# Sixteen more gate halves between the stick-breaking turns, two casts on another engine, four gate halves at a stage switch

## The chip, the cores and the metric

The kernel runs as one program on one core of a Trainium2 chip. The number that counts is the device time of one execution in microseconds. Three runs of the kernel before took 2511.12, 2511.8 and 2515.66 us, so the median is 2511.8 us. Everything is fp32, but each large product is computed from three fp32r products of a high and a low half (below), so one logical matmul is three instructions on TensorE.

## The reference, cut to what matters

The model is two blocks one after the other. The first (windowed attention, a gated delta rule, an FFN) is not touched. The second, `hybrid_layer`, normalizes, projects `h` to eleven pieces, runs three mixers, and merges them with three sigmoid gates:

```
h = rms_norm(x, g_pre);  u = h @ w_in            # 1024 tokens, 1024 -> 5120 + 3 * 1024 columns
y_pool = pool_mixer(pool_v) * silu(pool_g)       # branch one,   1024 x 512
y_conv = conv_mixer(conv_x, ...) * silu(conv_g)  # branch two,   1024 x 512
y_sb   = stick_breaking(q, k, v) * silu(sb_g)    # branch three, 1024 x 512
proj   = branches[n] @ w_branch[n]               # 512 -> 1024, for n = 0, 1, 2
merged = sum over n of sigmoid(merge[n]) * proj[n]
out    = x + rms_norm(merged @ w_out, g_post)
```

`merge` is the last 3 * 1024 columns of `u`: one gate of 1024 x 1024 for each branch. A gate depends on `h` alone, not on its branch, so it can be computed at any time after `h`. Stick-breaking attention walks for each of 8 heads over blocks of 128 keys from the last to the first and needs at each block the sum of the blocks after it, so it is a chain:

```
logits = q @ k * scale;  log_keep = where(mask, log_sigmoid(-logits), 0)
later  = reversed cumsum of log_keep, less log_keep
weights = where(mask, exp(log_sigmoid(logits) + later), 0);  out = weights @ v
```

## The kernel before, in words

Matrices stand transposed: a tile has 128 rows of features and 512 tokens, and a "half" is one of the two runs of 512 tokens. A weight tile of 128 x 512 is loaded by `weight` (line 103: the DMA on SyncE's queue, line 106), split into a high part `wh` (a cast) and a low part `wl` (a subtraction on GpSimd), and used by `mm3` (lines 147 to 149), three matmuls of 128 x 128 by 128 x 512. A flag, `busy[0]`, says which engine casts: ScalarE outside the stick-breaking stage (line 98), VectorE inside it (line 109).

Two stages matter here.

**The stick-breaking stage.** Sixteen streams (`stream`: 8 heads, each for two halves of the queries) run two at a time in turns. A stream has 4 or 8 key blocks, together 96, and a block passes `logits` (two matmuls into `l`, then copy, Abs, Exp and Ln on ScalarE, line 990 on VectorE), `closing` (lines 998, 1000 and 1001 on VectorE), `sums` (two matmuls into `S`), `weights` (VectorE adds at line 1011, ScalarE takes Exp at line 1012, VectorE casts to `uh` at line 1014, GpSimd subtracts to `ul` at line 1015) and `values` (two matmuls into `O`). A block is 128, 256, 384 or 512 queries wide; 48 of the 96 have all 512. Between turns the generator `others` gives TensorE other work in steps of three matmuls of 512 columns: the projections and activations of branches one and two, the gate of stick-breaking and, for `AHEAD` = 8 tiles of 128 gate rows (two halves each), the whole gate of branch one, which goes to DRAM (`ga_d`). That makes 576 steps, and 8 more sets of three in the pooling epilogue. There are 272 turns; the first 24 steps and the last 24 stand apart, and the others are spread evenly over the turns:

```
while turn[1] and done < LEAD + (t + 1) / len(turns) * (total - LEAD - SPARE):
    next(fill, None)
```

TensorE's order in this stage is as written. The order of all other engines, and TensorE's elsewhere, comes from the framework's scheduler.

**The merge stage.** For each branch `n`, eight tiles `Y[k, h]` (4 blocks of 128 features, two halves) are loaded through two `yr` buffers, for `n` = 2 multiplied by the gate `sg_d` on GpSimd (line 1188, with both buffers in use), and split into high and low (ScalarE line 98, VectorE line 99). Their pool holds ten pairs: eight in use and two ahead. Then for each of 8 row tiles `m` and two halves: a gate half (24 matmuls, and a sigmoid: ScalarE lines 156, 158, 159, VectorE line 157) or, for branch one, a load of it from `ga_d` into `s` (line 1198); then 12 matmuls of `Y`; then VectorE multiplies by the gate, and for `n` > 0 GpSimd adds to the sum (line 1212). In all, 16 x 12, 16 x 36 and 16 x 36 matmuls for the three branches. SyncE issues all loads in one queue, in order.

Of the kernel before, what the change touches and what calls it, by code (L numbers as in the profile page):

```python
# [9 lines left out]
F32 = mybir.dt.float32  # L10
# [7 lines left out]
P = 128  # L18
# [38 lines left out]
def tile_hybrid_layers(ctx, tc, a, out):  # L57
    nc = tc.nc
    act, dve, gp, pe, sp = nc.scalar, nc.vector, nc.gpsimd, nc.tensor, nc.sync
    dma = sp.dma_start  # L60
# [36 lines left out]
    def split(H, L, src, eng=None):  # L97
        act.copy(H, src)  # L98
        (eng or dve).tensor_sub(L, src, f32(H))  # L99

    busy = [False]

    def weight(src, n=1):

        raw = wp.tile([P, 512], F32, name="raw", tag="raw", bufs=3)
        dma(raw.rearrange("p (k m) -> p k m", k=n), src.rearrange("(k p) m -> p k m", p=P))
        H, L = (wp.tile([P, 512], F32R, name=f"w{q}", tag=f"w{q}", bufs=8) for q in "hl")
        if busy[0]:
            dve.tensor_copy(H, raw)  # L109
            gp.tensor_sub(L, raw, f32(H))  # L110
        else:
            split(H, L, raw, gp)
        return H, L
# [4 lines left out]
    def cols(W, c0, n, K=8):  # L118

        g = [weight(W[k * P : (k + n) * P, c0 : c0 + 512 // n], n) for k in range(0, K, n)]  # L120

        def tile_of(k, m):
            c = (k % n) * (512 // n) + m * P
            return tuple(x[:, c : c + P] for x in g[k // n])

        return tile_of
# [18 lines left out]
    def mm3(ps, A, B, first, last, asl=slice(None), bsl=slice(None)):  # L145

        pe.matmul(ps, A[0][:, asl], B[0][:, bsl], start=first, stop=False)  # L147
        pe.matmul(ps, A[0][:, asl], B[1][:, bsl], start=False, stop=False)  # L148
        pe.matmul(ps, A[1][:, asl], B[0][:, bsl], start=False, stop=last)  # L149

    def acc512():
        return pm[0].tile([P, 512], F32, name="mm", tag="mm")

    def sigmoid(s, x):

        act.activation(s, x, AF.Exp, scale=-1.0)
        dve.tensor_scalar(s, s, 1e18, 1.0, op0=ALU.min, op1=ALU.add)
        act.activation(s, s, AF.Ln)
        act.activation(s, s, AF.Exp, scale=-1.0)
# [176 lines left out]
    raw = wp.tile([P, 512], F32, name="raw", tag="raw", bufs=3)  # L336
# [6 lines left out]
    ps = bank()  # L343
# [7 lines left out]
    for h in range(2):  # L351
        ps = acc512()
# [28 lines left out]
    ps = bank()  # L381
# [10 lines left out]
    ps = bank()  # L392
# [38 lines left out]
    for c in range(8):  # L431
        kT = chunk_of(gk_d, c, "kT")
        ps = bank()
# [17 lines left out]
        b = up_tile("b", 2)  # L451
# [7 lines left out]
    for d in range(2):  # L459
# [3 lines left out]
        for b in range(4):  # L463
            r = slice(32 * b, 32 * b + 32)
# [4 lines left out]
        for s in range(1, 32):  # L469
            i = 31 - s if d == 0 else s  # L470
            r = slice(i + 1, 32) if d == 0 else slice(0, i)
            m = M.rearrange("p a b -> p (a b)")[:, : s * s].rearrange("p (a b) -> p a b", a=s)
# [3 lines left out]
        for b in range(4):  # L476
            r = slice(32 * b, 32 * b + 32)
# [9 lines left out]
    ps = bank()  # L487
# [15 lines left out]
    for c in (0, 7, 1, 6, 2, 5, 3, 4):  # L503
        vT = chunk_of(gv_d, c, "kT")
        ps = bank3()
# [7 lines left out]
    for c in (0, 7, 1, 6, 2, 5, 3, 4):  # L513
        kT, qT = chunk_of(gk_d, c, "kT"), chunk_of(gq_d, c, "qT")
        ps = bank2()
# [161 lines left out]
    for kv in range(2):  # L677
# [8 lines left out]
        for n in range(8):  # L686
# [12 lines left out]
            for h in range(4):  # L699
                ps = acc512()  # L700
# [21 lines left out]
            for b in range(nb):  # L722
                ps = bank()
                for h in range(4):
                    pe.transpose(ps[:, hs(h)], S[:, h, hs(b)], ident)
                H, L = (ap_.tile([P, 512], F32R, name="PT", tag="PT", bufs=4) for _ in range(2))
# [21 lines left out]
    for n in range(2):  # L748
        g = [rows(WO, k, 512 * n) for k in range(4)]
        for i in range(8):  # L750
# [4 lines left out]
            ps = acc512()  # L755
# [96 lines left out]
    HH = kts(HU)  # L852
# [111 lines left out]
    def stream(hd, half):  # L964

        r = slice(64 * hd, 64 * hd + 64)
        qc = slice(512 * half, 512 * half + 512)
        (K, V), Q = heads[hd], queries[hd, half]
        kbs = list(range(4 * half + 3, -1, -1))
        N = len(kbs)  # L970
        cut = [slice(max(0, P * kb - 512 * half), 512) for kb in kbs]
        st = {}

        def logits(j):

            kb, cs = kbs[j], cut[j]
            l = pl.tile([P, 512], F32, name="l", tag="l")
            for n in range(2):
                pe.matmul(l[:, cs], K[:, P * kb : P * kb + P], Q[n][:, cs], start=n == 0, stop=n == 1)
            u, e = ct("u", bufs=5), ct("e", bufs=3)  # L980
            c = cs.start
            if kb >= 4 * half:
                dve.tensor_add(u[:, c : c + P], l[:, c : c + P], neg2)
                c += P
            if c < 512:
                act.copy(u[:, c:], l[:, c:])
            act.activation(e[:, cs], u[:, cs], AF.Abs)
            act.activation(e[:, cs], e[:, cs], AF.Exp, scale=-1.0)
            act.activation(e[:, cs], e[:, cs], AF.Ln, bias=one)
            dve.scalar_tensor_tensor(e[:, cs], u[:, cs], 0.0, e[:, cs], op0=ALU.max, op1=ALU.add)  # L990
            st[j] = u, e

        def closing(j):

            (u, e), cs = st[j], cut[j]
            if j:
                cp = cut[j - 1]
                dve.tensor_sub(e[96:97, cp], e[96:97, cp], Sb[0][0:1, cp])
            eH, eL = ct("eh", F32R, EB), ct("el", F32R, EB)
            dve.tensor_copy(eH[:, cs], e[:, cs])  # L1000
            dve.tensor_sub(eL[:, cs], e[:, cs], f32(eH[:, cs]))
            st[j] = u, (eH, eL)

        def sums(j):
            Sb[0] = pS.tile([P, 512], F32, name="S", tag="S")
            for n, x in enumerate(st[j][1]):
                pe.matmul(Sb[0][:, cut[j]], upto, x[:, cut[j]], start=n == 0, stop=n == 1)

        def weights(j):
            u, cs = st[j][0], cut[j]  # L1010
            dve.tensor_add(u[:, cs], u[:, cs], Sb[0][:, cs])
            act.activation(u[:, cs], u[:, cs], AF.Exp)
            uH, uL = ct("uh", F32R), ct("ul", F32R)
            dve.tensor_copy(uH[:, cs], u[:, cs])  # L1014
            gp.tensor_sub(uL[:, cs], u[:, cs], f32(uH[:, cs]))  # L1015
            st[j] = st[j] + ((uH, uL),)

        def values(j):
            for x in st.pop(j)[2]:
                pe.matmul(Ob[:, cut[j]], V[:, kbs[j]].rearrange("p s d -> p (s d)"), x[:, cut[j]], start=False, stop=True,  # L1020
                          skip_group_check=True)

        Sb = [None]
        logits(0)
        yield
        yield
        for j in range(1, N + 1):
            closing(j - 1)
            if j < N:
                logits(j)  # L1030
            yield
            if j == 2:
                Ob = pO.tile([P, 512], F32, name="O", tag="O")
                dve.memset(Ob, 0.0)
            if j >= 2:
                values(j - 2)
            sums(j - 1)
            weights(j - 1)
            yield
        values(N - 1)  # L1040
        t = tmp()
        act.copy(t[0:64], Ob[64:128])
        dve.tensor_add(t[0:64], t[0:64], Ob[0:64])
        put(ys_d[r, qc], t[0:64])
# [25 lines left out]
            gp.tensor_mul(x, x, y)  # L1070
        put(dst, x)

    AHEAD, LEAD, SPARE = 8, 24, 24
    ga_d = scratch("ga_d", [AHEAD * P, T])

    def others():
# [98 lines left out]
    yp = pool(s7, "y")  # L1175
    gt = pool(s7, "gt")
    ac = pool(s7, "acc", 16)
    A = {}
    for n in range(3):
        Y = {}  # L1180
        for h in range(2):
            for k in range(4):
                raw = gt.tile([P, 512], F32, name="yr", tag="yr", bufs=2)
                dma(raw, y_d[n][k * P : (k + 1) * P, 512 * h : 512 * h + 512])
                if n == 2:
                    raw2 = gt.tile([P, 512], F32, name="yr", tag="yr", bufs=2)
                    dma(raw2, sg_d[k * P : (k + 1) * P, 512 * h : 512 * h + 512])
                    gp.tensor_mul(raw, raw, raw2)  # L1188
                Y[k, h] = tuple(yp.tile([P, 512], F32R, name="y", tag="y", bufs=20) for _ in range(2))
                split(*Y[k, h], raw)  # L1190
        for m in range(8):
            ahead = n == 0 and m < AHEAD
            gw = None if ahead else cols(W2, 5120 + 1024 * n + P * m, 4)
            bw = cols(a["w_branch_2"][0][n], P * m, 4, K=4)
            for h in range(2):
                s = gt.tile([P, 512], F32, name="s", tag="s", bufs=4)
                if ahead:
                    dma(s, ga_d[m * P : (m + 1) * P, 512 * h : 512 * h + 512])
                else:
                    ps = acc512()  # L1200
                    for k in range(8):
                        mm3(ps, gw(k, 0), HH[k][h], k == 0, k == 7)
                    sigmoid(s, ps)
                ps = acc512()
                for k in range(4):
                    mm3(ps, bw(k, 0), Y[k, h], k == 0, k == 3)
                if n == 0:
                    A[m, h] = ac.tile([P, 512], F32, name="a", tag="a")
                    dve.tensor_mul(A[m, h], ps, s)
                else:  # L1210
                    dve.tensor_mul(s, ps, s)  # L1211
                    gp.tensor_add(A[m, h], A[m, h], s)  # L1212
# [60 lines left out]
```

## Time and profile before

| | |
|---|---|
| median of three runs | 2511.8 us |
| the profiled execution | 2522.66 us, span 2520.9 us, mean granted clock 0.983 |
| TensorE busy | 2384.3 us (95%), 11098 matmuls |
| VectorE, ScalarE, GpSimd busy | 1285.9, 1074.3, 928.8 us |
| stick-breaking stage | from about 1542 to 2119 us |
| merge stage | 2119 to about 2425 us |
| output projection and final norm | to the end |

Times in rows are microseconds from the span's start. PE is TensorE, PEld its weight loads, DVE VectorE, ACT ScalarE, POOL GpSimd, SP SyncE; a `q` behind an engine's name is its instruction queue. A matmul row's duration is from its start to the end of its last result, so rows of consecutive matmuls overlap.

### The profile page before, as it was taken

What the parts mean: (1) busy time and instruction counts of PE and PEld (TensorE: products, weight loads), DVE (VectorE), ACT (ScalarE), POOL (GpSimd) and SP (SyncE); (2) the same over time, 40 slices, a digit from 0 to 9 for tenths busy, and PEclk for the clock granted to TensorE, in tenths of its full rate; (3) what the DMA queues carried; (4) which work ended last, traced back from release to release, by engine and by line L of the source; (5) the groups of instructions that cost most, each with busy time, mean ns of one, the idle gap of its engine ahead of it and who ended that gap; (6) DMA issues with size and microseconds to landing.
All of it is one profiled execution on the core that took longest, in us unless ns stands there. A gap on an engine that the chain in (4) does not pass through costs nothing. (4 is left out here: it accounts for less than half of the span.)

```text
span 2520.9 us, 31629 instructions
## 1 busy us (share of the span) xinstructions
PE 2384.3 (95%) x11098; PEld 1954.2 (78%) x11098; DVE 1285.9 (51%) x2481; ACT 1074.3 (43%) x2185; POOL 928.8 (37%) x799
## 2 busy tenths in 40 slices
PE   7899888899999999999999999998999999999998
PEld 5677677887788888888888788777777787888887
DVE  5579936885632211221123504999888885312113
ACT  5554215664542233223224423666555575333331
POOL 3344224434332222222223214455444442345354
PEclk9999988999999999999999999999999999999999
DMA  5895795656221111111112324122222225312123
GB/s 164 226 286 170 214 289 159 195 150 203 73 69 57 42 43 51 50 50 51 50 51 92 103 89 121 57 76 66 66 67 64 71 80 171 113 51 84 51 72 121
DMA packets 307282, 268.47 MB, mean 106 GB/s; under 512 B 44871, under 2 KB 240387, under 8 KB 307123
## 3 DMA queue, kind: packets, MB, share of 16 engines
q1 hardware_dynamic: 264403, 213.41, 29.6%
q10 hardware_dynamic: 42720, 53.05, 6.1%
q8 instruction: 87, 1.43, 0.2%
q14 instruction: 72, 0.59, 0.1%
HBM read 203.92 MB, written 64.57 MB: 107 GB/s over the span
## 5 line engine op out<-in xcount | busy, mean ns | idle before, releaser
L99 POOL TENSOR_TENSOR wl<-raw,wh 128x512 fp32r<-128x512 f32 x276 | 370.8, 1355 | 834.8 <-ACT wh L98 808.9
L147 PE MATMUL mm<-uh,wh 128*128 128x512 f32 x1472 | 578.3, 393 | 0.2 <-DVE mx L1066 0.2
L149 PE MATMUL mm<-uh,wl 128*128 128x512 f32 x1472 | 576.9, 392 | 0.0
L148 PE MATMUL mm<-ul,wh 128*128 128x512 f32 x1472 | 576.4, 392 | 0.0
L98 ACT CAST wh<-raw 128x512 fp32r<-128x512 f32 (+1 forms) x277 | 169.9, 618 | 460.9 <-PE mm L149 239.3
L149 PEld LDWEIGHTS mm<-uh,wl 128*128 128x128 f32 x1472 | 277.7, 189 | 59.5
L147 PEld LDWEIGHTS mm<-uh,wh 128*128 128x128 f32 x1472 | 278.1, 189 | 55.0 <-DVE mx L1066 0.6
L148 PEld LDWEIGHTS mm<-ul,wh 128*128 128x128 f32 x1472 | 277.8, 189 | 55.4
L99 DVE TENSOR_TENSOR hid<-t,hid 128x512 fp32r<-128x512 f32 x64 | 55.4, 866 | 310.1 <-ACT hid L98 310.1
L149 PE MATMUL mm<-wh,hid 128*128 128x512 f32 x512 | 199.0, 389 | 0.0
L148 PE MATMUL mm<-wl,hid 128*128 128x512 f32 x512 | 198.8, 389 | 0.0
L147 PE MATMUL mm<-wh,hid 128*128 128x512 f32 x512 | 198.7, 389 | 0.0
L845 DVE TENSOR_TENSOR h<-h,mm 128x512 f32<-128x512 f32 x128 | 87.9, 687 | 212.3 <-PE mm L149 212.2
L1015 POOL TENSOR_TENSOR ul<-u,uh 128x512 fp32r<-128x512 f32 (+3 forms) x96 | 106.1, 1106 | 134.5 <-DVE uh L1014 108.5
L147 PE MATMUL mm<-xnh,wh 128*128 128x512 f32 x352 | 142.6, 405 | 11.1 <-ACT cv L280 5.8
L110 POOL TENSOR_TENSOR wl<-raw,wh 128x512 fp32r<-128x512 f32 x72 | 101.6, 1411 | 120.7 <-DVE wh L109 45.2
L148 PE MATMUL mm<-xnl,wh 128*128 128x512 f32 x352 | 141.8, 403 | 0.0
L149 PE MATMUL mm<-xnh,wl 128*128 128x512 f32 x352 | 141.4, 402 | 0.0
L148 PEld LDWEIGHTS mm<-wl,hid 128*128 128x128 f32 x512 | 96.1, 188 | 20.0
L147 PEld LDWEIGHTS mm<-wh,hid 128*128 128x128 f32 x512 | 96.1, 188 | 20.0
L149 PEld LDWEIGHTS mm<-wh,hid 128*128 128x128 f32 x512 | 96.1, 188 | 19.9
L830 ACT ACTIVATE t<-mm 128x512 f32<-128x512 f32 x64 | 38.2, 597 | 149.8 <-PE mm L149 149.8
(331 smaller groups left out, 4616.3 us busy)
## 6 DMA issues: line engine op xcount, KB each, us to landing
raw<-in_w_in SPq DMA_DIRECT2D x172, 256.0 KB
raw<-in_w_ffn_in SPq DMA_DIRECT2D x64, 256.0 KB
raw<-in_w_ffn_out SPq DMA_DIRECT2D x64, 256.0 KB
e<-e_d SPq DMA_DIRECT2D x16, 512.0 KB
raw<-in_w_out SPq DMA_DIRECT2D x32, 256.0 KB
kv<-kv_d SPq DMA_DIRECT2D x16, 512.0 KB
kT<-gk_d SPq DMA_DIRECT2D x30, 256.0 KB
raw<-in_w_branch SPq DMA_DIRECT2D x24, 256.0 KB
```

Source lines behind the costliest of these rows:

```text
L98: act.copy(H, src)
L99: (eng or dve).tensor_sub(L, src, f32(H))
L110: gp.tensor_sub(L, raw, f32(H))
L147: pe.matmul(ps, A[0][:, asl], B[0][:, bsl], start=first, stop=False)
L148: pe.matmul(ps, A[0][:, asl], B[1][:, bsl], start=False, stop=False)
L149: pe.matmul(ps, A[1][:, asl], B[0][:, bsl], start=False, stop=last)
L830: act.activation(t, ps, AF.Relu)
L845: dve.tensor_add(Hs[order[p], n], Hs[order[p], n], ps)
L1015: gp.tensor_sub(uL[:, cs], u[:, cs], f32(uH[:, cs]))
```

## The change

`AHEAD` goes from 8 to 16: the stick-breaking stage also computes the whole gate of branch two and stores it in `ga_d`, and the merge stage loads it. In that stage the cast of `weight` alternates between VectorE and ScalarE, and the cast to `uh` moves to ScalarE. At the start of the merge stage, behind the splits of branch one's `Y`, four gate halves of branch three (row tiles 0 and 1) are computed and kept in four `se` buffers until branch three uses them.

```diff
-    busy = [False]
+    busy = [False, False]
...
         if busy[0]:
-            dve.tensor_copy(H, raw)
+            busy[1] = not busy[1]
+            dve.tensor_copy(H, raw) if busy[1] else act.copy(H, raw)
             gp.tensor_sub(L, raw, f32(H))
...
             uH, uL = ct("uh", F32R), ct("ul", F32R)
-            dve.tensor_copy(uH[:, cs], u[:, cs])
+            act.copy(uH[:, cs], u[:, cs])
...
-    AHEAD, LEAD, SPARE = 8, 24, 24
+    AHEAD, LEAD, SPARE = 16, 24, 24
...
+    def gate(gw, h, tag, bufs):
+        s = gt.tile([P, 512], F32, name="s", tag=tag, bufs=bufs)
+        ps = acc512()
+        for k in range(8):
+            mm3(ps, gw(k, 0), HH[k][h], k == 0, k == 7)
+        sigmoid(s, ps)
+        return s
+
+    EARLY = (2, 0), (2, 1)
...
+        if n == 0:
+            for b, m in EARLY:
+                gw = cols(W2, 5120 + 1024 * b + P * m, 4)
+                for h in range(2):
+                    E[b, m, h] = gate(gw, h, "se", 4)
         for m in range(8):
-            ahead = n == 0 and m < AHEAD
-            gw = None if ahead else cols(W2, 5120 + 1024 * n + P * m, 4)
+            ahead = 8 * n + m < AHEAD
+            gw = None if ahead or (n, m) in EARLY else cols(W2, 5120 + 1024 * n + P * m, 4)
...
                 if ahead:
-                    dma(s, ga_d[m * P : (m + 1) * P, 512 * h : 512 * h + 512])
+                    s = gt.tile([P, 512], F32, name="s", tag="s", bufs=4)
+                    r = (8 * n + m) * P
+                    dma(s, ga_d[r : r + P, 512 * h : 512 * h + 512])
                 else:
-                    ps = acc512()
-                    for k in range(8):
-                        mm3(ps, gw(k, 0), HH[k][h], k == 0, k == 7)
-                    sigmoid(s, ps)
+                    s = E[n, m, h] if gw is None else gate(gw, h, "s", 4)
```

The first place is ScalarE's queue in the stick-breaking stage. Before, it holds the Exp of `weights` (L1012) among the passes for the next logits (`e`) and the fill's sigmoid (`mx`):

```order
L988 ACTIVATE e_14988<-e_14988 128x512
L1012 ACTIVATE u_14896<-u_14896 128x384
L989 ACTIVATE e_14988<-e_14988,cc_75 128x512
L158 ACTIVATE mx_15001<-mx_15001 128x512
L986 COPY u_15035<-l_15032 128x256
```

Now the cast to `uh` (L1015) and a weight cast (L110) stand in the same queue:

```order
L1013 ACTIVATE u_13029<-u_13029 128x384
L990 ACTIVATE e_13145<-e_13145,cc_75 128x512
L1015 CAST uh_13165<-u_13029 128x384
L110 CAST wh_13655<-raw_13653 128x512
L157 ACTIVATE mx_13207<-mm_13132 128x512
```

The Exp and the cast of one block are now on one engine, with one pass of the next block between them; VectorE's queue no longer has the cast.

The second place is TensorE's queue at the change from branch two to branch three in the merge stage. Before, the last `Y` matmuls of branch two (mm_19419) are followed by the first gate half of branch three (mm_19525, from `uh` and `ul`, 24 matmuls):

```order
L147 MATMUL mm_19419<-y_18566,wh_19340 128x512
L148 MATMUL mm_19419<-y_18567,wh_19340 128x512
L149 MATMUL mm_19419<-y_18566,wl_19341 128x512
L147 MATMUL mm_19525<-uh_11321,wh_19508 128x512
L148 MATMUL mm_19525<-ul_11322,wh_19508 128x512
```

Now the `Y` matmuls of branch three follow at once: tile 0's first half (12, not shown), one matmul of its second half (mm_19719, from pair 4), tile 1's first half (mm_19740, 12), and behind it one matmul of its second half (mm_19755) and the first six of the gate of tile 2 (mm_19789). From the last of mm_19740 on:

```order
L150 MATMUL mm_19740<-y_19658,wl_19737 128x512
L148 MATMUL mm_19755<-y_19667,wh_19736 128x512
L148 MATMUL mm_19789<-uh_11321,wh_19772 128x512
L149 MATMUL mm_19789<-ul_11322,wh_19772 128x512
L150 MATMUL mm_19789<-uh_11321,wl_19773 128x512
L148 MATMUL mm_19789<-uh_11321,wh_19772 128x512
L149 MATMUL mm_19789<-ul_11322,wh_19772 128x512
L150 MATMUL mm_19789<-uh_11321,wl_19773 128x512
L149 MATMUL mm_19719<-y_19668,wh_19700 128x512
```

y_19658 is `Y` pair 3 of branch three, y_19667 and y_19668 are pair 4. Between the first matmul that needs pair 4 and the first that needs pair 5 stand 29 matmuls, and 22 each from pair 5 to pair 6 and from pair 6 to pair 7.

## Rows read from the trace of the kernel before

**Rows 1.** Busy time by stage: length, PE, PEld, DVE, ACT, POOL (instructions), granted clock.
```profile
1542.00:2119.00 577.00, 536.49 (x2329) 424.06 (x2328) 492.89 (x878) 344.21 (x677) 281.11 (x236) 0.99 0.27 79
2119.00:2163.00 44.00, 44.00 (x196) 36.44 (x195) 15.82 (x21) 10.29 (x18) 11.62 (x9) 1.00 0.53 167
2163.00:2294.00 131.00, 131.00 (x580) 108.47 (x579) 31.02 (x40) 46.43 (x79) 55.53 (x43) 1.00 0.24 73
2294.00:2425.00 131.00, 130.12 (x575) 107.28 (x574) 26.43 (x35) 51.52 (x89) 64.60 (x50) 1.00 0.19 59
```

**Rows 2.** Timeline of PE in the merge stage: start, duration.
```profile
2129.99 0.39 PE L149 MATMUL mm<-y,wl 128*128 128x512 f32 x1
...
2151.07 0.39 PE L149 MATMUL mm<-y,wl 128*128 128x512 f32 x1
```

**Rows 3.** Waits of PE, 1542 to 2119: us in total, times, longest.
```profile
PE S L1007 <- DVE el L1001: 14.4, 22, 1.9
PE O L1020 <- POOL ul L1015: 10.2, 16, 1.5
```

**Rows 4.** Groups of DVE instructions, 1542 to 2119: count, busy, mean ns, idle before.
```profile
L1001 DVE TENSOR_TENSOR el<-e,eh 128x512 fp32r<-128x512 f32 x48 | 47.7, 995 | 0.9
L109 DVE CAST wh<-raw 128x512 fp32r<-128x512 f32 x66 | 41.3, 626 | 4.0 <-PE mm L148 2.4 <-DMA raw<-in_w_in 0.9
L990 DVE SCALAR_TENSOR_TENSOR e<-u,e 128x512 f32<-128x512 f32 x48 | 39.3, 819 | 9.5 <-ACT e L989 9.4
L1011 DVE TENSOR_TENSOR u<-u,S 128x512 f32<-128x512 f32 x48 | 32.6, 680 | 3.8 <-PE S L1007 3.5
L1000 DVE CAST eh<-e 128x512 fp32r<-128x512 f32 x48 | 31.1, 648 | 0.3
L1014 DVE CAST uh<-u 128x512 fp32r<-128x512 f32 x48 | 29.1, 605 | 6.0 <-ACT u L1012 5.6 <-issue 0.2
L157 DVE TENSOR_SCALAR mx<-mx 128x512 f32<-128x512 f32 x39 | 25.2, 647 | 5.7 <-ACT mx L156 5.6
L998 DVE TENSOR_TENSOR e<-e,S 1x512 f32<-1x512 f32 x32 | 21.8, 682 | 1.0
```

**Rows 5.** Instructions on tiles mx, on raw, of L1014, same stretch: DVE, ACT, POOL busy.
```profile
1542.00:2119.00 577.00, 93.24 (x131) 80.88 (x133) 11.55 (x8) 0.99 0.27 79
...
1542.00:2119.00 577.00, 40.75 (x66) 3.67 (x6) 102.31 (x73) 0.99 0.27 79
...
1542.00:2119.00 577.00, 54.35 (x96) 0.99 0.27 79
```

**Rows 6.** Groups of ACT instructions in that stretch.
```profile
L989 ACT ACTIVATE e<-e,cc 128x512 f32<-128x512 f32 x48 | 34.5, 720 | 2.4 <-DVE eh L1000 0.9 <-POOL mx L1070 0.5
L987 ACT ACTIVATE e<-u 128x512 f32<-128x512 f32 x48 | 30.2, 630 | 1.8 <-POOL mx L1070 0.7 <-ACT u L986 0.3
L98 ACT CAST Q<-t 128x512 fp32r<-128x512 f32 x16 | 9.9, 618 | 14.8 <-DVE t L1043 10.3 <-DMA t<-sq_d 4.5
```

**Rows 7.** Timeline of DVE: start, duration.
```profile
1998.88 1.23 DVE L109 CAST wh<-raw 128x512 fp32r<-128x512 f32 x1
...
2001.86 0.41 DVE L1000 CAST eh<-e 128x512 fp32r<-128x512 f32 x1
```

**Rows 8.** The chain that ended last, from branch two to branch three: start, duration.
```profile
2285.87 0.24 PE mm L149
...
2288.26 1.26 POOL yr L1188
2289.55 0.63 ACT y L98
...
2294.76 1.28 POOL yr L1188
...
2315.36 1.30 POOL yr L1188
```

**Rows 9.** All waits of PE from 2119 to 2425.
```profile
PE mm L147 <- ACT y L98: 0.9, 1, 0.9
```

More of the change, by code (lines that the diff above doesn't have):

```diff
@@ L1177, in tile_hybrid_layers @@
     ac = pool(s7, "acc", 16)
-    A = {}
+    A, E = {}, {}
+    def gate(gw, h, tag, bufs):
[6 more added lines that the diff above has]
+    EARLY = (2, 0), (2, 1)
     for n in range(3):
@@ L1190, in tile_hybrid_layers @@
                 split(*Y[k, h], raw)
+        if n == 0:
[3 more added lines that the diff above has]
+                    E[b, m, h] = gate(gw, h, "se", 4)
         for m in range(8):
-            ahead = n == 0 and m < AHEAD
-            gw = None if ahead else cols(W2, 5120 + 1024 * n + P * m, 4)
+            ahead = 8 * n + m < AHEAD
+            gw = None if ahead or (n, m) in EARLY else cols(W2, 5120 + 1024 * n + P * m, 4)
             bw = cols(a["w_branch_2"][0][n], P * m, 4, K=4)
             for h in range(2):
-                s = gt.tile([P, 512], F32, name="s", tag="s", bufs=4)
                 if ahead:
-                    dma(s, ga_d[m * P : (m + 1) * P, 512 * h : 512 * h + 512])
-                else:
-                    ps = acc512()
-                    for k in range(8):
-                        mm3(ps, gw(k, 0), HH[k][h], k == 0, k == 7)
-                    sigmoid(s, ps)
+                    s = gt.tile([P, 512], F32, name="s", tag="s", bufs=4)
+                    r = (8 * n + m) * P
+                    dma(s, ga_d[r : r + P, 512 * h : 512 * h + 512])
+                else:
+                    s = E[n, m, h] if gw is None else gate(gw, h, "s", 4)
                 ps = acc512()
```

## The prediction

> **What bounds the kernel now.** I read the busy time by stage first [rows 1], since the change touches only the stick-breaking stage and the merge stage. In the merge stage PE never rests: 44.00 of 44 us, 131.00 of 131, 130.12 of 131, and all its waits there come to 0.9 us [rows 9]. So that stage lasts as long as its matmuls, and a matmul taken out of it is time taken out.
>
> What a matmul costs is read from starts, not from durations: from 2129.99 to 2151.07 there are 93 intervals without a gap [rows 2], so 21.08 / 93 = 0.2267 us each, though each row says 0.39. A step of three costs 0.680 us.
>
> With that price the stick-breaking stage looks different. Its 2329 matmuls [rows 1] are 584 x 3 = 1752 of fill and 96 x 6 = 576 of the streams. The streams' have 4608 columns per head and operand set (1280 for four blocks, 3328 for eight), times 6 matmuls and 8 heads, as much as 432 full ones. So PE needs (1752 + 432) x 0.2267 = 495 us and the stage lasts 577: 82 us are lost. The busy column leaves only 577 - 536.5 = 40.5 us [rows 1], since it counts the overlapping tail of each matmul. The Trainium skill (Trainium Kernel Development and Optimization, Best Practices) says not to judge by the busy share of matmuls; the trace agrees, 40.5 against 82. By the busy column the sum below would come out near no change; by the count it does not.
>
> The views then say who keeps PE waiting. The waits name the low half of `closing` on DVE, 14.4 us, and `ul`, 10.2 us, whose cast is on DVE before GpSimd subtracts [rows 3]. DVE is busy 492.9 of 577 us, ACT 344.2, POOL 281.1 [rows 1].
>
> Averages hide the cause, because blocks differ in width. For a block of 512 queries DVE needs 0.995 + 0.819 + 0.680 + 0.648 + 0.605 + 0.682 = 4.43 us [rows 4]. The fill adds (93.24 + 40.75) / 584 = 0.229 us a step [rows 5], and a block has two turns of (576 - 48) / 272 = 1.94 steps, so 3.88 steps: 0.89. Together 5.32 us. PE needs for the same block 3.88 x 0.680 + 6 x 0.2267 = 4.00. DVE is short by 1.32 us in each of 48 such blocks, 63 of the 82 us. The other 19 us are short waits of other kinds.
>
> **The change part by part.**
>
> *Branch two's gate.* 16 halves x 24 = 384 matmuls x 0.2267 = 87.0 us leave the merge stage and 128 steps, the same 87.0 us, enter the stick-breaking stage. They save nothing by themselves; they save what they fill. In the merge stage 16 loads of `s` on SyncE's queue replace them. Branch one already runs with such loads beside 12 matmuls a half, at 167 GB/s, with PE at 44.00 of 44 [rows 1], so I cost them at nothing. Their stores add 16 issues to ACT's queue among hundreds of instructions. Upper end for both: one more wait like branch three's below, 9 us.
>
> *The casts.* From DVE go 54.35 us for `uh` [rows 5], and of 88 weight casts (72 before) 44 stay. To DVE come 16 more sigmoid passes of 0.647 [rows 4]. In a full block DVE now has 4.43 - 0.605 = 3.82, and of the fill (93.24 + 10.4 + 44 x 0.626) / 712 = 0.184 a step. A block now has 2 x (704 - 48) / 272 = 4.82 steps, so 0.89: 4.71 us. PE has 4.82 x 0.680 + 1.36 = 4.64. ACT has 0.720 for Ln, 0.630 for Abs, which I take for the other three passes too, and 0.618 for the cast, together 3.86 [rows 6], and of the fill, its passes at 0.63 again, (80.88 + 16 x 3 x 0.63 + 44 x 0.618) / 712 = 0.194 a step, 0.94: 4.79. So DVE is short by 0.07 us and ACT by 0.15, times 48: 3 and 7 us, where 63 stood.
>
> A cast on DVE has two prices: 0.41 us at 2001.86 and 1.23 at 1998.88 for the same shape [rows 7], with a mean of 0.605 to 0.648 [rows 4], against 0.618 on ACT [rows 6]. I use the means, since GpSimd keeps working. The Trainium skill (VectorE: DVE Perf Modes, Mode 2×_2P) speaks against the move: a copy of fp32 within SBUF can use both read ports and give two results a cycle, so it should be cheaper on DVE than anywhere. The trace shows that only in its best case, 0.41; what it would mean for the time is the fourth rival.
>
> *What stays lost in this stage.* 19 + 3 + 7 = 29 us. I take 36, because ACT and DVE are now short in the same blocks and a late result in one queue delays the other. The ends: 14 if most of the other 19 goes too, 82 if DVE's load was not the cause. PE's need becomes 582 us, so the stage takes 618, 41 more than before. Behind each cast on ACT stand the passes of both streams' next logits; who waits is `closing` on DVE, then `sums` on PE.
>
> *The four early halves.* They move 96 matmuls, 21.8 us, from the start of branch three to the start of the merge stage. No wait stands there now [rows 9], so they cover nothing new: 0. But they, with branch two's gate gone, uncover the change to branch three. Its `Y` pairs come one by one through two buffers: load, multiply on POOL, cast, subtract. Pairs 3 to 7 are multiplied at 2288.26 to 2315.36, so 27.1 / 4 = 6.8 us each, and a multiplication and a cast later (1.28 + 0.63) the first matmul may start [rows 8]. Counted from 2286.1, when the last but one `Y` half of branch two ends [rows 8], pair 4 is there at 10.6, then 17.4, 24.2 and 31.0. Before, 60 matmuls stood ahead of branch three's first `Y`, and 36 more ahead of pair 4. Now PE reaches pair 4 after 24 matmuls, 5.4 us: it waits 5.2. Then it has 29, 22 and 22 matmuls in between (6.6, 5.0 and 5.0 us), waits 0.2, 1.8 and 1.8. In all 9 us where 0.9 stood, so +8. Lower end 4, if pairs come as fast as the best; upper 27, if the gate of tile 2 can't fill its gaps. The change to branch two has no multiplication and one load for a pair; I take 0 there.
>
> *Sum.* Stick-breaking +41, merge -87 + 8 = -79: -38 us. The profiled execution took 2522.66 us (its span is 2520.9), so it would take 2485. The median of the runs is 10.9 us lower, and I subtract the same 38 there: 2474 us.
>
> **The rivals.**
>
> *All of it is filled* (lost 14, switch 4 us): -65, 2447. For it: 4.64 us of PE's work against 4.71 and 4.79 is nearly even, and narrower blocks have slack. Against: the 19 us.
>
> *ACT takes DVE's place* (lost 64): -18 + 8 = -10, 2502. For it: ACT gets about 55 us of `uh`, 27 of weight casts and 30 of sigmoids on top of 344.2, and has to serve both streams in order. Against: 456 of 618 us is 74%, where DVE was at 85%.
>
> *The wait was never DVE's load* but the length of the chain (lost 82): +8, 2520. Against: the Exp and its cast now follow on one engine, which shortens the chain too.
>
> *Casts on DVE were cheap* (0.41 us each, the best of [rows 7], lost 61). DVE's shortage would have been about 0.8 us a block, 38 us in all; some 44 of the 82 would have another cause and stay, with ACT's 7 and 10 for two late queues: -21 + 8 = -13, 2499. Against: the means of [rows 4].
>
> *Slower: weight casts block ACT.* A cast waits until PE gives a weight buffer back, and on ACT the next logits of both streams stand behind it. Its place is line 110 in the stick-breaking stage. At 1.3 us for each of 44 the lost time is 36 + 57 = 93: +19, 2531. It decides from about 1 us each, when 36 + 43 = 79 us are lost. Against: the same 66 casts on DVE waited 4.0 us in all [rows 4], 0.06 each.
>
> *A long wait at branch three* (27 us there): -38 + 18 = -20, 2492.
>
> **How the numbers follow.** Forecast 55%, with its own range 2456 to 2492; all filled 12%; ACT in DVE's place 13%; long wait at branch three 7%; cheap casts 3%; chain 5%; blocked ACT 5%. About 0.2%, 5 us, is what a measurement of this kernel can tell from no change. The chain and blocked cases are slower; of ACT in DVE's place I count a part as same. So faster 0.86, same 0.05, slower 0.09. The range of 8 in 10 runs from the filled case to a little past ACT's: 2448 to 2506.
>
> **What would show it.** Right: the stick-breaking stage about 618 us long with 2713 matmuls; DVE there near 436 us busy and ACT near 456; waits of `S` and `O` together under half of now; branch two in the merge stage 44 us long; one gap of about 5 us before pair 4 of branch three and two small ones. Wrong: ACT with hardly an idle moment and waits of `l` or `el` on it; weight casts on ACT with waits of a microsecond on PE; a stick-breaking stage of 650 us or more; gaps in branch two behind loads of `s`; or a wait at the start of the merge stage that the early halves hid.

## The result and the profile after

The changed kernel takes 2481.1 us (median of four runs, 2476.45 to 2483.46), against 2512.85 us before on the same chip: a ratio of 0.9873, with a 95% interval of 0.9858 to 0.9888, so some 32 us less. The forecast was 38 less, 2474 us.

The two profiled executions differ by more, 39.2 us of span. Nine of these lie ahead of anything that changed: the same matmul of the unchanged part, shortly before the fill begins, starts at 1542.34 us before and at 1533.26 after. From there on the change gave 30 us, and that agrees with the medians.

The busy time by stage answers to [rows 1]: from the start of the fill to the end of the stick-breaking stage, the four early halves, then branches one, two and three. The columns are length, PE, PEld, DVE, ACT, POOL (instructions in brackets), clock.

```profile
1533.00:2156.60 623.60, 605.64 (x2717) 494.99 (x2715) 465.31 (x776) 435.68 (x867) 299.41 (x253) 1.00 0.29 88
2156.60:2180.00 23.40, 23.40 (x96) 19.25 (x97) 3.73 (x5) 9.13 (x15) 4.64 (x4) 0.93 0.26 78
2180.00:2223.60 43.60, 43.60 (x194) 36.08 (x194) 13.31 (x18) 7.99 (x13) 10.33 (x8) 1.00 0.48 147
2223.60:2267.90 44.30, 43.78 (x193) 35.94 (x192) 16.53 (x23) 8.72 (x15) 33.01 (x26) 1.00 0.60 185
2267.90:2386.50 118.60, 112.33 (x481) 91.71 (x480) 23.01 (x32) 42.54 (x73) 61.67 (x49) 0.96 0.20 62
```

The stick-breaking stage went from 577 to 623.6 us (+46.6) and took in 87.0 us of matmuls. The merge stage went from 306 to 229.9 us (-76) and lost the same 87.0. So the first saved 41 us and the second gave 11 back. Branch two, which was 131 us long, runs in 44.3 us with its gates loaded.

The waits of PE in the stick-breaking stage, after the change (total, times, longest), answer to [rows 3]:

```profile
PE O L1021 <- POOL ul L1016: 3.9, 5, 0.8
PE l L980 <- ACT u L987: 3.1, 4, 1.0
PE mm L148 <- ACT mx L157: 2.7, 1, 2.7
PE S L1008 <- DVE el L1002: 2.6, 3, 1.2
```

The wait for `el` fell from 14.4 to 2.6 us, that for `ul` from 10.2 to 3.9. A new one of 2.7 us, for ScalarE, stands third; it lies at the switch of stages, before the first early half, and is explained under the run with four `yr` buffers.

The groups of DVE in that stage answer to [rows 4], and the last two rows, of ACT, are the casts that moved there:

```profile
L1002 DVE TENSOR_TENSOR el<-e,eh 128x512 fp32r<-128x512 f32 x48 | 51.3, 1069 | 0.9
L158 DVE TENSOR_SCALAR mx<-mx 128x512 f32<-128x512 f32 x56 | 38.8, 693 | 15.0 <-ACT mx L157 14.1 <-DMA raw<-in_w_branch 0.3
L1001 DVE CAST eh<-e 128x512 fp32r<-128x512 f32 x48 | 38.0, 791 | 0.9
L991 DVE SCALAR_TENSOR_TENSOR e<-u,e 128x512 f32<-128x512 f32 x48 | 37.5, 782 | 26.9 <-ACT e L990 26.6
L110 DVE CAST wh<-raw 128x512 fp32r<-128x512 f32 x41 | 21.7, 529 | 9.5 <-PE mm L149 7.7 <-DMA y_d<-mx 1.5
...
L1015 ACT CAST uh<-u 128x512 fp32r<-128x512 f32 x48 | 29.6, 617 | 3.0 <-PE O L1021 0.6 <-DVE u L984 0.5
L110 ACT CAST wh<-raw 128x512 fp32r<-128x512 f32 x41 | 25.2, 614 | 6.9 <-PE mm L149 3.0 <-DMA raw<-in_w_in 2.8 <-PE S L1008 0.9
```

The moved casts cost 0.617 and 0.614 us, as forecast. The cast that stayed on DVE, `eh`, rose from 0.648 to 0.791 us and `el` from 0.995 to 1.069. DVE did get idle time: 26.9 us before line 991, where it had 9.5.

All waits of PE from the early halves to the end of branch three, after the change, the 2.7 us of the switch among them once more; before, there was one of 0.9 us [rows 9]:

```profile
PE mm L148 <- ACT y L98: 5.6, 2, 4.0
PE mm L148 <- ACT mx L157: 2.7, 1, 2.7
PE mm L149 <- DVE y L99: 0.6, 1, 0.6
PE mm L148 <- DVE s L1226: 0.5, 1, 0.5
```

The timeline of PE at the change to branch three shows where the 5.6 us lie and what follows them (start, duration, then the idle time before):

```profile
2271.76 0.50 PE L148 MATMUL mm<-y,wh 128*128 128x512 f32 x1 [1.64 <-ACT y L98]
2272.89 0.80 PE L149 MATMUL mm<-y,wh 128*128 128x512 f32 x1 [0.63 <-DVE y L99]
...
2278.11 1.22 PE L148 MATMUL mm<-y,wh 128*128 128x512 f32 x2 [3.99 <-ACT y L98]
2279.12 0.63 PE L149 MATMUL mm<-y,wh 128*128 128x512 f32 x1
2279.55 0.63 PE L150 MATMUL mm<-y,wl 128*128 128x512 f32 x1
...
2283.53 0.40 PE L148 MATMUL mm<-y,wh 128*128 128x512 f32 x1
```

From 2279.12 to 2279.55 it is 0.43 us from one matmul's start to the next, not 0.2267: the granted clock was at the lower of its two levels, 1.2 GHz, from 2272.9 to 2283.2 us, after the waits of 1.64 and 0.63 us. The first two waits are for pair 3 of `Y`, the third is for pair 4; pairs 5 to 7 came in time.

### The profile page after: what moved, and what is told of

It reads as the page before. It is cut to its first block, busy times and chain, and to the rows that moved or that the text cites. A ratio compares the mean times of both kernels' runs of the same rounds, so it can differ in the third digit from the quotient of the medians.

```text
span 2481.7 us, 31649 instructions
## 1 busy us (share of the span) xinstructions
PE 2368.2 (95%) x11098; PEld 1953.0 (79%) x11098; DVE 1241.2 (50%) x2357; ACT 1127.4 (45%) x2309; POOL 925.2 (37%) x799
## 5 line engine op out<-in xcount | busy, mean ns | idle before, releaser
L98 ACT CAST wh<-raw 128x512 fp32r<-128x512 f32 (+1 forms) x261 | 159.9, 618 | 446.5 <-PE mm L150 241.3
```

## The experiments

Two questions were open: which part of the change took the waits out of the stick-breaking stage, and what the early halves cost. For each run "lost" is the length of the stick-breaking stage, from one and the same matmul near its start to the first matmul of the next stage, less its matmuls at 0.2267 us per 512 columns; "lost later" is the same from there to the last `Y` matmul.

| kernel | median us | ratio to before, 95% | lost | lost later |
|---|---|---|---|---|
| before | 2512.9, 2510.7, 2509.2 | 1 | 82 | 1 |
| changed | 2481.1 | 0.9873 (0.9858 to 0.9888) | 41 | 12.5 |
| gates alone | 2498.4 | 0.9940 (0.9921 to 0.9959) | 59 | 5.5 |
| casts alone | 2497.4 | 0.9944 (0.9924 to 0.9964) | 68 | 0 |
| no early halves | 2474.0 | 0.9837 (0.9813 to 0.9862) | 41 | 4.7 |
| four yr buffers | 2471.4 | 0.9836 (0.9814 to 0.9857) | 37 | 0.1 |
| ... and only uh moved | 2474.7 | 0.9862 (0.9844 to 0.9879) | 46 | 0.1 |
| ... and only weights moved | 2482.7 | 0.9890 (0.9871 to 0.9909) | 49 | 0.1 |
| four yr, AHEAD 20, no early | 2466.3 | 0.9823 (0.9807 to 0.9839) | 36 | 0 |
| four yr, AHEAD 24, no early | 2458.6 | 0.9797 (0.9781 to 0.9814) | 29 | 0 |

The three medians of before belong to the three chips: the first to the changed kernel, the second to the next four, the third to the last four. The lost times come from one profiled execution each, so a difference of a few microseconds between two of them says little.

Lost time is not all waiting. Taken matmul by matmul from the starts in the traces, the lost time of the stick-breaking stage has three parts: what PE loses at its idle times, what it loses at the lower clock, and the rest, in which it neither waits nor runs at the lower clock (matmuls of 512 columns start 0.230 to 0.231 us apart there on average, and the narrow ones cost more than their share of columns).

| kernel | lost | idle | lower clock | the rest |
|---|---|---|---|---|
| before | 82 | 56 | 6 | 20 |
| gates alone | 59 | 37 | 4 | 18 |
| casts alone | 68 | 46 | 4 | 18 |
| changed | 41 | 23 | 2 | 16 |
| four yr, AHEAD 24, no early | 29 | 13 | 0 | 16 |

**The gates alone.**

```diff
-            busy[1] = not busy[1]
-            dve.tensor_copy(H, raw) if busy[1] else act.copy(H, raw)
+            dve.tensor_copy(H, raw)
...
-            act.copy(uH[:, cs], u[:, cs])
+            dve.tensor_copy(uH[:, cs], u[:, cs])
...
-    EARLY = (2, 0), (2, 1)
+    EARLY = ()
```

> Branch two's gate moved (AHEAD 16), both casts back on VectorE, no early halves. If VectorE's load in full-width blocks was the wait (theory): VectorE needs 4.43 + 4.82 x 0.223 = 5.50 us a full block against TensorE's 4.64, short 0.86 x 48 = 41 us, with the other 19 about 60 us lost in the stick-breaking stage: about 2492 us, VectorE again the busiest engine beside TensorE and named by TensorE's waits. If more fill between the turns is enough by itself (rival): the lost time is about 40 us as in the changed kernel, and without the early halves the time is about 2472 us.

Measured: 2498.4 us and 59 us lost, where the theory said 60 and the rival 40; 2.6 of the 59 lie at the switch of stages. More fill between the turns is not enough by itself. DVE again has the highest load beside PE:

```profile
1541.00:2179.30 638.30, 608.68 (x2699) 491.14 (x2697) 515.91 (x911) 377.66 (x727) 299.63 (x251) 0.99 0.28 85
```

515.9 us of DVE in 638.3 is 81%; in the changed kernel it is 465.3 in 623.6, 75%. But PE's waits name DVE less than the theory asked. The largest two are for GpSimd and ScalarE, and the wait for `el` is 2.3 us where it was 14.4:

```profile
PE O L1020 <- POOL ul L1015: 8.6, 10, 1.6
PE l L979 <- ACT u L986: 6.6, 8, 1.7
PE S L1007 <- DVE eh L1000: 3.3, 3, 1.6
...
PE S L1007 <- DVE el L1001: 2.3, 6, 0.6
```

**The casts alone.**

```diff
-    AHEAD, LEAD, SPARE = 16, 24, 24
+    AHEAD, LEAD, SPARE = 8, 24, 24
...
-    EARLY = (2, 0), (2, 1)
+    EARLY = ()
```

> Both casts moved as in the change, but AHEAD stays 8 and there are no early halves. Theory (VectorE's load): VectorE needs 4.59 us and ScalarE 4.54 us a full block against TensorE's 4.00, so some 28 us of shortage instead of 63, with the rest 45 to 60 us lost instead of 82: 2478 to 2490 us. Rival (the waits are the length of the chain, only more fill covers them): within 5 us of before, 2508 to 2518 us.

Measured: 2497.4 us and 68 us lost, between the two. So the rival that the casts do nothing falls, but the theory asked too much of them. DVE went from 85% to 79% (442.3 of 559.9 us), and still PE waited 14.5 us for `el`, as before:

```profile
PE S L1008 <- DVE el L1002: 14.5, 20, 2.1
PE O L1021 <- POOL ul L1016: 8.1, 11, 1.6
```

Set beside the gates alone this tells more: there DVE was busier (81%) and the wait for `el` went all but away, here DVE is freer and the wait stays. So it was the longer fill, 4.82 steps a block for 3.88, that covered the chain up to `el`, and not the freer DVE. The two parts saved 23 and 14 us of lost time apart and 41 together, close to a sum.

**No early halves.**

```diff
-    EARLY = (2, 0), (2, 1)
+    EARLY = ()
```

> The change without the four early halves. Theory (they cover nothing at the start of the merge stage and uncover the change to branch three): TensorE has 72 matmuls, 16.3 us, before it needs pair 4 of branch three and its 7.8 us of waits there go, with the slow clock after them: 8 to 10 us less than the changed kernel, about 2472 us; the wait of 2.9 us at the start of the merge stage stays, before the first matmul on y. Rival (they cover a wait for branch one's y at the switch of stages): a wait of 5 us or more appears at the start of the merge stage and the time is 2481 us or more.

Measured: 2474.0 us. By the ratios to before this is 9 us less than the changed kernel (0.9837 against 0.9873; the intervals overlap a little), and by the two profiles 7 us less are lost (46 against 53, both stages together). The waits after the stick-breaking stage began, in this kernel:

```profile
PE mm L148 <- ACT mx L157: 3.5, 1, 3.5
PE mm L148 <- ACT y L98: 1.9, 1, 1.9
```

No wait for branch one's `y` came up: the 3.5 us are the wait of the switch that the changed kernel has too, now in front of the first `Y` matmul, and branch three keeps one wait of 1.9 us.

**Four yr buffers.**

```diff
-                raw = gt.tile([P, 512], F32, name="yr", tag="yr", bufs=2)
+                raw = gt.tile([P, 512], F32, name="yr", tag="yr", bufs=4)
...
-                    raw2 = gt.tile([P, 512], F32, name="yr", tag="yr", bufs=2)
+                    raw2 = gt.tile([P, 512], F32, name="yr", tag="yr", bufs=4)
```

> The changed kernel with four yr buffers instead of two. Theory (the pairs of branch three come one by one because load, multiplication and split share two buffers): the next pair's loads run beside the split, pairs come in about 3.5 us instead of 5.8 to 6.8, TensorE waits 2 us or less there instead of 7.8; at the start of the merge stage the loads no longer hold ScalarE's queue and the 2.9 us before the first early half go too: about 2470 us. Rival (the pace is set by the shared loads of weights and s in SyncE's queue, not by the buffers): pairs stay 5.5 us or more apart and the time stays 2479 to 2484 us.

Measured: 2471.4 us, and nothing lost after the stick-breaking stage, early halves included. The multiplications of branch three's last three pairs on POOL in this kernel (start, duration):

```profile
2268.15 1.29 POOL L1200 TENSOR_TENSOR yr<-yr 128x512 f32<-128x512 f32 x1 [0.69 <-POOL a L1227]
2270.64 1.75 POOL L1200 TENSOR_TENSOR yr<-yr 128x512 f32<-128x512 f32 x1
2275.31 1.30 POOL L1200 TENSOR_TENSOR yr<-yr 128x512 f32<-128x512 f32 x1
```

and in the changed kernel, with two buffers:

```profile
2281.94 1.28 POOL L1200 TENSOR_TENSOR yr<-yr 128x512 f32<-128x512 f32 x1 [4.54 <-DMA yr<-sg_d]
2287.46 1.29 POOL L1200 TENSOR_TENSOR yr<-yr 128x512 f32<-128x512 f32 x1 [0.89 <-DMA yr<-sg_d]
2293.11 1.29 POOL L1200 TENSOR_TENSOR yr<-yr 128x512 f32<-128x512 f32 x1 [4.37 <-DMA yr<-sg_d]
```

These come 5.6 us apart behind a DMA; with four buffers it is 2.5 and 4.7, and none of them waits for a load. For these pairs the buffers set the pace, not SyncE's queue. The wait at the switch shrank to 1.0 us: with two buffers ScalarE stood at a cast of `y` that waited for its load, and behind it in the queue stood the Exp of the last fill gate, for which PE's next stage waited. The timeline of ACT in the changed kernel:

```profile
2154.89 0.62 ACT L98 CAST y<-yr 128x512 fp32r<-128x512 f32 x1 [1.13 <-DMA yr<-y_d]
2155.41 0.61 ACT L98 CAST wh<-raw 128x512 fp32r<-128x512 f32 x1
2155.93 0.59 ACT L157 ACTIVATE mx<-mm 128x512 f32<-128x512 f32 x1
```

PE's first early matmul starts at 2156.57, when that Exp is done.

**Only one of the two casts**, on the kernel with four `yr` buffers.

```diff
# only uh on ScalarE
-            busy[1] = not busy[1]
-            dve.tensor_copy(H, raw) if busy[1] else act.copy(H, raw)
+            dve.tensor_copy(H, raw)
# only the weights alternate
-            act.copy(uH[:, cs], u[:, cs])
+            dve.tensor_copy(uH[:, cs], u[:, cs])
```

> As the run with four yr buffers, but all weight casts of the stick-breaking stage on VectorE again; only the uh cast is on ScalarE. Theory (VectorE's and ScalarE's load in full-width blocks): VectorE 3.82 + 4.82 x 0.223 = 4.89 us, ScalarE about 4.6 against TensorE's 4.64, short 12 us, so some 38 to 45 us lost in the stage instead of 37: 0 to 8 us over the run with four yr buffers. Rival (VectorE's load counts wherever it is, so each microsecond taken from it is worth the same; the two casts took 54 and about 21 to 28 us): about a third of the difference of 22 us between the gates alone (59 us lost) and the whole change is due to the weight casts, 44 to 45 us lost, 7 us over.

Measured: 2474.7 us, 46 us lost, 9 more than with both. That is 1 us above the upper end of both the theory (38 to 45) and the rival (44 to 45), so it doesn't tell them apart; the times, 2471.4 and 2474.7 on two chips, do not settle it either.

> As the run with four yr buffers, but the uh cast is on VectorE again; only half the weight casts are on ScalarE. Theory: VectorE 4.43 + 0.89 = 5.32 us a full block against TensorE's 4.64, short 33 us, with the other 19 about 52 us lost: 15 us over the run with four yr buffers. Rival (it is not the load but the chain: Exp and its cast on one engine save a hand-over for ul): the lost time is as with the gates alone, 59 us, 22 us over.

Measured: 2482.7 us, 49 us lost: near the theory's 52, and not the 59 of a hand-over that alone counts. From 59 lost, `uh` takes 13, the weights take 10, and both together 22; in each of the three savings 1.5 us come from the shorter wait at the switch (2.6 us there, 1.1 with four buffers). The weight casts are no part of the chain, so this run shows that DVE's queue matters and not the chain alone. Which of the two casts is worth more per microsecond stays open: the lost times differ by 3 us, the medians of the two kernels, on one chip, by 8.

**More fill still.**

```diff
-    AHEAD, LEAD, SPARE = 16, 24, 24
+    AHEAD, LEAD, SPARE = 20, 24, 24     # and 24
...
-    EARLY = (2, 0), (2, 1)
+    EARLY = ()
```

and four `yr` buffers.

> Four yr buffers, no early halves, and AHEAD 20: half of branch three's gate is computed in the stick-breaking stage too, 64 more steps. Theory (time is lost there while TensorE has less work in a full block than VectorE and ScalarE): TensorE has 5.29 x 0.68 + 1.36 = 4.96 us a full block against 4.9 of ScalarE and 4.8 of VectorE, no shortage is left, about 30 us lost instead of 37: 7 us under the run with four yr buffers, less 0 to 5 us of waits at branch three, which now has no gate to fill its gaps: 2464 to 2471 us. Rival (what is left lost are single waits that more fill doesn't cover): no change, 2471 to 2476 us.

> As the run with AHEAD 20, with AHEAD 24: all three gates are computed in the stick-breaking stage, 64 steps more. Theory: TensorE 5.76 x 0.68 + 1.36 = 5.28 us a full block, about 26 us lost there; the merge stage is branch matmuls alone: 2460 to 2470 us. Rival: lost time as in the run with four yr buffers, and waits for loads in branch three: 2471 to 2480 us.

Measured: 2466.3 and 2458.6 us. The second is the fastest kernel of the study, 0.9797 of before, its interval (0.9781 to 0.9814) clear of the changed kernel's; it lies 1.4 us under the range that was given for it. Branch three has no gate left that could fill gaps, and needs none: no time is lost after the stick-breaking stage in either. In that stage 36 and 29 us are lost (30 and 26 expected). With AHEAD 24 the stage and the merge stage look so:

```profile
1541.00:2235.70 694.70, 683.88 (x3082) 562.59 (x3081) 483.76 (x799) 473.40 (x919) 317.67 (x266) 1.00 0.30 91
2235.70:2366.00 130.30, 130.30 (x576) 107.95 (x575) 46.22 (x62) 31.54 (x52) 87.65 (x69) 1.00 0.54 172
```

DVE and ACT are at 70% and 68%, and the merge stage is 576 matmuls without a gap. The step from 16 to 20 saved one microsecond of lost time by these single profiles, the step to 24 seven more; how the saving divides between the two steps is within what profiles of one execution can differ.

## Why the prediction was right

**The bound.** PE's count of matmuls against the stage's length gave 82 us that could be won, where the busy column showed 40.5. The change won 41 us in that stage and AHEAD 24 won 53, more than 40.5: the count was the better measure. But not all of the 82 could be won: 20 of them are neither waits nor lower clock, and 16 of these are still there with AHEAD 24, so the bound is nearer 62 to 66.

**Who made PE wait.** The forecast put 63 of the 82 us down to DVE in full-width blocks. The gates alone lose 59 us with DVE's load left high (60 by the same sum), but the casts alone lose 68 and not 45 to 60. The sum takes whatever is longer, PE's or DVE's work of a block, and has no term for the length of the chain, which the wait for `el` in these two runs shows to be there. It also reads DVE too high. PE's price is taken from start to start, DVE's from rows, and back-to-back rows of DVE overlap by 0.08 us (ACT's by 0.09 to 0.10): in the stage before, DVE's durations add up to 534 us in 492.9 us busy. Six such rows a block are up to 0.48 us, an estimate of up to 23 of the 63 us. (Line 998, too, runs at full width in 32 of the 48 blocks only [rows 4], 2 us less.) And the other 19 us were not short waits of other kinds: 20 us are no waits at all, and 6 are the lower clock, which stood for 17 us of the stage before and 3.4 after. So the split into 63 and 19 isn't shown. What is shown is that more fill and less load on DVE each took part of the waits.

**Lost time after.** 41 us against 36 in the forecast; 2.9 of them, from start to start, are the wait at the switch. That it came so near is in part luck: the 36 hold 7 us that no row gave, and the 19 and the 63 behind it were something else, as said. DVE was to be busy 436 us and was 465. `eh` and `el` became slower by 0.14 and 0.07 us a block, and the full-width chain on DVE costs 1.069 + 0.791 + 0.782 + 0.680 + 0.682 = 4.00 us, with line 998's 0.682 unchanged, not 3.82: 0.18 x 48 = 9 us more. Of the other 20, 13 are the overlap again: a cast that leaves doesn't take its whole duration out of DVE's busy time (durations fell by 41 us, busy time by 28). The rest lies in the narrower blocks and in `mx`. ACT, at 436 us, stayed under the 456 forecast; it did not become the new bound.

**Branch two.** 44.3 us with 0.5 us of wait: sixteen more loads of `s` cost nothing there, as forecast. Some of them stood ahead of a load of branch three, as said next.

**The early halves.** "They cover nothing new: 0" and +8 at branch three was the right sign; without them the kernel is faster by about 7 to 9 us. The size was a little off. The waits at branch three sum to 7.1 us (9 forecast, 0.9 before), but the lower clock behind them, 10.2 us long, cost about 3 more; and the wait of 2.9 us before the first early matmul with 3.4 us of lower clock after it, 1.7 lost, had no term. Pair 3 was late too, by 1.64 us, where I had counted it in time, and pairs 5 to 7, which were to cost 3.8 us, came in time. The multiplication of pair 3 waited for its second load, which SyncE issued 13 us after the first:

```profile
2253.14 0.32 SPq L1196 DMA_DIRECT2D yr<-y_d  x1
...
2266.08 0.38 SPq L106 DMA_DIRECT2D raw<-in_w_in  x1
2266.55 0.46 SPq L1199 DMA_DIRECT2D yr<-sg_d  x1
...
2269.79 1.26 POOL L1200 TENSOR_TENSOR yr<-yr 128x512 f32<-128x512 f32 x1 [1.24 <-DMA yr<-sg_d]
```

Between them the queue held weights and `s`, each of which waited for a buffer that GpSimd's sums and splits gave back. So for pair 3 SyncE's queue, and GpSimd behind it, did set the time.

**The sum.** Stick-breaking +46 (+41 forecast), merge -76 (-79): -30 in the profiles, -32 in the medians, against -38. The mechanism was right in its main lines: what was moved saves nothing by itself, fill and freer DVE shorten PE's waits, and the early halves cost. The mis-sized terms are the lost time, 41 for 36, and the two switches, 12.5 lost for 9 after the stick-breaking stage.

**The rivals.** The blocked ACT queue did not come in the stage: weight casts on ACT waited 6.9 us in all, 0.17 each, where 1 us was needed. A small form of it did stand at the switch, with casts of `y` in place of weight casts. Cheap casts on DVE fall as well: 0.41 us was again only the best case, and the means of `eh` rose. That all is filled (14 lost) was out of reach: 16 us stay lost without any wait even with AHEAD 24. The chain's length as the only cause falls by the run with only the weights moved; as one cause of two it stands. The long wait at branch three (27 us) did not come: 7.1.

What stays open: why matmuls of the stick-breaking stage start 0.004 us later than in the merge stage where nothing is waited for, and what the 13 us of idle time are that AHEAD 24 leaves, where neither DVE nor ACT is at more than 70%.

## What to carry to other kernels

Judge a stage that TensorE shares with a chain by counting its matmuls at their start-to-start price, and count the other engines' work the same way, in the widest turns and not on average. Whether the chain is too long or an engine too full, runs of each remedy alone help to tell: here more fill and less load on VectorE both shortened the waits, and their savings nearly added. When independent work is moved away from a stage, ask what it was hiding there: the loads at the next change of data need another buffer before the cover goes, or the gain is partly given back. Work put ahead of time at a place where nothing waits gains nothing and takes cover from where it stood.

## What the hardware showed that was not expected

The `eh` cast of 128 x 512 that stayed on VectorE rose from 0.648 to 0.791 us on average. It was not the other casts' leaving that raised it: in the gates-alone kernel, where none left, it is 0.772, with the casts alone 0.789 and with AHEAD 24 0.819. The traces show what the slow ones have in common: they begin while GpSimd is at an instruction.

```profile
2077.76 1.30 POOL L99 TENSOR_TENSOR wl<-raw,wh 128x512 fp32r<-128x512 f32 x1
2077.97 1.38 DVE L1000 CAST eh<-e 128x512 fp32r<-128x512 f32 x1
```

This is from the kernel before; the cast at 2001.86 [rows 7], with GpSimd idle, took 0.41. In these five kernels 93 of the 240 full-width `eh` casts began with no GpSimd instruction running (or one in its last 0.1 us), and every one took 0.41 to 0.43 us. The other 147 began beside one, and 141 of them took 0.46 to 1.54. Before the change 23 of 48 began so, after it 35. The addition at line 1011 before (1012 after), which reads the matmuls' result `S`, kept 0.67 to 0.69 us either way. The Trainium skill (GPSIMD Engine Reference, 1. Specifications) states that GpSimd shares its SBUF interfaces with VectorE and contends with instructions that have two SBUF inputs or run in a two-port mode. The traces agree for the cast; no run took GpSimd's work away, so this stays an observation and not an experiment.

The lower clock came after short waits in the merge stage: 10.2 us at half speed after waits of 1.64 and 0.63 us, through a further wait of 3.99, and 3.4 us after one of 2.74. In the kernel with four buffers, where the waits at these places are 1.0 us and none, neither came.
